# A two-layer decoder trunk: the first gate/up products queued behind the whole output projection, and a norm's matmuls queued one product later

## The chip, the core and the metric

One program runs on one core of one Trainium2 chip. Its engines work side by side, each on its own queue in program order: TensorE (PE for matrix products, with the loading of its stationary operand shown apart as PEld), VectorE (DVE), ScalarE (ACT), GpSimd (POOL) and SyncE (SP, which here only issues transfers). The metric is the device time of one execution in microseconds (us); lower is better.

## What is computed

A trunk of two layers over 512 tokens of width 1024, all in 32-bit floats. Each layer mixes tokens (attention of two kinds), adds the mix through an output projection, and adds a gated feed-forward block. The mixers matter here only as what comes before; the places of the change are the last two lines of the loop.

```python
for layer in range(2):
    mix = mixer(rmsnorm(x, attn_norm_g[layer]), ...)    # 512 x 1024
    x = x + mix @ w_out[layer]                          # output projection, 1024 x 1024
    h = rmsnorm(x, ffn_norm_g[layer])                   # the feed-forward norm
    g, u = jnp.split(h @ w_gate_up[layer], 2, axis=-1)  # 1024 x 5632
    x = x + (jax.nn.silu(g) * u) @ w_down[layer]        # 2816 x 1024
return rmsnorm(x, final_norm_g)
```

## The kernel before

**Products.** Every large matrix product is made from split operands: `hi` is the value rounded for TensorE, `lo` the rest, and a product is three matmuls (hi·hi, lo·hi, hi·lo). ACT makes `hi` (a cast), DVE makes `lo` (a subtraction). In the output projection two of the four weight pieces of a column block get `lo` in another way: ACT writes the negated weight and a POOL transfer adds to it.

**Output projection** (`out_proj`, `project`, lines 199 to 201). It works in four blocks of 256 output columns, `o` = 0 to 3, in the PSUM bank pairs `acc`, `sc`, `y`, `tr`. A block has 48 matmuls of 512 columns and uses four weight chunks (`whi`, `wlo`). After block `o` DVE adds the residual (lines 603, 604), ACT and DVE make the feed-forward operands of these columns: the split halves `xh`, `xl` and the sums `sh`, `sl` (line 608, `make`, lines 565 to 568, and `split`, lines 228 and 229). In layer 1 the new residual is also turned to token rows: four transposes for each 128 columns (line 619), which are traced one block later, and copied by ACT (line 620), with squares summed for the norm (line 625).

**Feed-forward** (`ffn`, `quad`). Eleven quads of 256 gate and 256 up columns. Each uses a seven-product scheme (a Strassen-like form): products `a11`, `s3`, `s2`, `s1`, `a22`, `a12`, `s4`, each with 24 matmuls of 256 columns (lines 835 to 837), in four contraction blocks `e` = 0 to 3, where `e` needs the columns that block `o = e` of the output projection made. For quad 0 the weights of the first three products are loaded and split ahead (`FirstThree`), and the first three products are traced in two parts: `e` = 0 to 2 of all three, then `e` = 3. They write the banks `acc`, `y` and `sc`, while block 3 of the projection writes `tr`. The down projection of an earlier quad fills places in later quads (`fill`, lines 934 to 936 in layer 1).

**The norm.** The products run on unnormalised operands; the row factor `r1` is multiplied in later (lines 900 and 902). In layer 0 it comes from `finish_norm`, in layer 1 from `norm_of_rows` (lines 630 to 638): a short chain on ACT and DVE, four products with a matrix of ones on PE (line 637), and a copy to `r1` on ACT (line 638).

**What sets the order.** The program is traced, and a scheduler then reorders each engine's instructions by its own model of their times, keeping the data dependences. `with behind(engine):` adds an edge: what the block traces on that engine stays behind the last instruction traced on it so far. On the chip each engine then runs its own row in the order given, and an instruction that waits holds all behind it.

Of the kernel before, what the change touches and what calls it, by code (L numbers as in the profile page):

```python
# [34 lines left out]
def tile_yoco(  # L35
# [68 lines left out]
    def behind(engine):  # L104

        e = engine.engine
        return tc.issue_after(next(i for i in reversed(nc.cur_bb.bb.instructions) if i.engine == e))
# [427 lines left out]
    NP = NKB // 2  # L535
# [91 lines left out]
    def norm_of_rows(ss):  # L627

        r = tmp("nrm", (P, NT))
        dve.tensor_add(ss[:, 0], ss[:, 0], ss[:, 1])  # L630
        rstd(ss[:, 0], NT, D, r)
        dve.tensor_scalar_mul(r, r, undo_k(D))
        d = work().rearrange("p (t c) -> p t c", c=P)
        b = bank("tr")
        for t in range(NT):
            dve.tensor_scalar_mul(d[:, t], ident, r[:, t : t + 1])
            pe.matmul(b[:, t * P : (t + 1) * P], ones, d[:, t], start=True, stop=True)
        act.copy(r1, b)
# [183 lines left out]
    def ffn(l, acc, last, qs, late, ring, sc, pl, ahead):  # L822
        raw, parts = ring.load, ring.parts
        wg = w_gate_up[l].rearrange("(e two p) c -> two p e c", two=2, p=P)
        wd = w_down[l].rearrange("(j p) c -> p j c", p=P)

        def product(b, form, w, es=range(NP)):

            hi, lo = w
            for u in range(2):  # L830
                o = b[:, u * H : (u + 1) * H]
                uc = slice(u * P, (u + 1) * P)
                for e in es:
                    ah, al = qs.operand(form, e)
                    pe.matmul(o, hi[:, e, uc], ah, start=u == 0 and e == 0, stop=False)  # L835
                    pe.matmul(o, lo[:, e, uc], ah, start=False, stop=False)  # L836
                    pe.matmul(o, hi[:, e, uc], al, start=False, stop=u == 1 and e == NP - 1)  # L837

        def halves(t):
            return t.rearrange("p (u c) -> p u c", u=2)  # L840

        gated = {}
        if last:
            ss = tmp("ss", (P, 2, NT))
            row_squares(qs.rows(), ss, 0)

        def quad(q, down):

            gc, uc = slice(q * 256, q * 256 + 256), slice(DFF + q * 256, DFF + q * 256 + 256)
            d = [next(down, None) for _ in range(4)]  # L850

            def fill(i):
                if d[i]:
                    d[i]()

            first, second = slice(0, H), slice(H, S)
            w = ahead[0] if q == 0 else FirstThree(l, q, ring)
            b11, t1 = w.b11, w.t1
            b21, b22 = raw(wg[1][:, :, gc]), raw(wg[1][:, :, uc])
            bp1, bp7, bp6 = bank("acc"), bank("y"), bank("sc")  # L860
            if q == 0:
                for es in (range(NP - 1), range(NP - 1, NP)):
                    product(bp1, "a11", w.w11, es)
                    product(bp7, "s3", w.wt3, es)
                    product(bp6, "s2", w.wt2, es)
                with behind(pe):
                    if last:
                        for f in late:
                            f()
                        row_squares(qs.rows(), ss, 1)  # L870
                    else:
                        finish_norm(acc, False, bank("tr"))
            else:
                product(bp1, "a11", w.w11)
                product(bp7, "s3", w.wt3)
                fill(0)
                product(bp6, "s2", w.wt2)
            p1, u2, u3 = sc.half("p1"), sc.half("u2"), sc.half("u3")
            g, u = sc.full("g"), sc.full("u")
            g1, g2, v1, v2 = g[:, :, first], g[:, :, second], u[:, :, first], u[:, :, second]  # L880
            act.copy(p1, bp1)
            dve.tensor_add(u2, bp6, p1)
            dve.tensor_add(u3, bp7, u2)
            bp5 = bank("acc")
            product(bp5, "s1", parts(t1))
            dve.tensor_sub(v2, halves(bp5), halves(u3))
            dve.tensor_sub(v1, halves(bp5), halves(u2))
            fill(1)
            if q == 0 and last:
                with behind(pe):  # L890
                    norm_of_rows(ss)
            dve.tensor_add(b11, b11, b21)
            bp4 = bank("y")
            product(bp4, "a22", parts(b11))
            dve.tensor_add(g2, halves(bp4), halves(u3))
            bp2 = bank("sc")
            product(bp2, "a12", parts(b21))
            dve.tensor_add(g1, halves(bp2), halves(p1))
            rr = r1.unsqueeze(1).to_broadcast([P, 2, S])
            dve.tensor_mul(g, g, rr)  # L900
            act.activation(g, g, AF.Silu)
            dve.tensor_mul(g, g, rr)
            fill(2)
            bp3 = bank(("acc", "y")[q % 2])
            product(bp3, "s4", parts(b22))
            dve.tensor_add(v1, halves(bp3), v1)
            fill(3)
            dve.tensor_mul(u, u, g)
            ah, al = (pl.tile([P, 2, S], F32R, tag=t, name=nm(t), bufs=4) for t in ("ah", "al"))
            split(u, ah, al)  # L910
            gated[q] = ah, al

        GROUPS = [(0,), (1, 2), (3, 4), (5, 6), (7, 8), (9, 10)]

        def blocks_of(group):
            return [(h[:, i], l_[:, i]) for q in group for h, l_ in (gated[q],) for i in range(2)]

        def down_blocks(group):

            k0, nk = 2 * group[0], 2 * len(group)  # L920
            w = {}

            def piece(i):
                a = blocks_of(group)
                c = i // 2
                if i % 2 == 0:
                    w[c] = parts(raw(wd[:, k0 : k0 + nk, c * 256 : c * 256 + 256], shape=(P, nk, 256)))
                hi, lo = w[c]
                b = bank("tr")
                if last:  # L930
                    for t in (2 * (i % 2), 2 * (i % 2) + 1):
                        tc_, o = slice(t * P, (t + 1) * P), b[:, (t % 2) * H : (t % 2) * H + H]
                        for k, (h, l_) in enumerate(a):
                            pe.matmul(o, h[:, tc_], hi[:, k], start=t % 2 == 0 and k == 0, stop=False)  # L934
                            pe.matmul(o, l_[:, tc_], hi[:, k], start=False, stop=False)  # L935
                            pe.matmul(o, h[:, tc_], lo[:, k], start=False, stop=t % 2 == 1 and k == nk - 1)  # L936
                    t0 = 2 * (i % 2)
                    dst = qs.rows()[:, t0 : t0 + 2, c * 256 : c * 256 + 256]
                    dve.tensor_add(dst, halves(b), dst)
                    return  # L940
                oc = slice((i % 2) * P, (i % 2) * P + P)
                for k, (h, l_) in enumerate(a):
                    pe.matmul(b, hi[:, k, oc], h, start=k == 0, stop=False)  # L943
                    pe.matmul(b, lo[:, k, oc], h, start=False, stop=False)  # L944
                    pe.matmul(b, hi[:, k, oc], l_, start=False, stop=k == nk - 1)  # L945
                if group != GROUPS[-1]:
                    dve.tensor_add(qs.block(i), b, qs.block(i))
                else:
                    xn = work()
                    dve.tensor_add(xn, b, qs.block(i))  # L950
                    split(xn, xh[:, i], xl[:, i])
                    squares(xn, nacc, i == 0)

            return [lambda i=i: piece(i) for i in range(8)]

        def all_down():
            for group in GROUPS[:-1]:
                yield from down_blocks(group)

        down = all_down()  # L960
        for q in range(NFF // 2):
            quad(q, down if q else iter(()))
        for f in down:
            f()
        exp_ln_tables()
        if not last:
            nacc = tmp("xacc")
            for f in down_blocks(GROUPS[-1]):
                f()
            return nacc  # L970
        k0 = 2 * GROUPS[-1][0]
        w = [[parts(raw(wd[:, k0 + k : k0 + k + 2, e * 512 : e * 512 + 512], shape=(P, 2, 512))) for k in (0, 2)] for e in range(2)]
        final(w, blocks_of(GROUPS[-1]), qs.rows(), ring, sc)
# [264 lines left out]
```

## Time and profile before

| | before |
|---|---|
| median of 3 runs | 1202.2 us (1201.6 to 1202.57) |
| profiled execution: time, span | 1206.7 us, 1204.9 us |
| mean granted clock of TensorE | 0.991 of 2.4 GHz |
| PE busy | 1168.8 us (97%) |
| PEld busy | 1064.8 us (88%) |
| DVE busy | 993.7 us (82%) |
| ACT busy | 662.8 us (55%) |
| POOL busy | 159.1 us (13%) |

The profiled execution took 1206.7 us, 4.5 us (0.4%) more than the median; its span runs from the first to the last instruction, and 1.8 us lie around it. Busy time is a sum of instruction durations, so an engine that is busy 97% of the span can still have stretches in which it stands still: these matter here. Layer 0's output projection ends near 273 us and its feed-forward runs to about 620 us; layer 1's output projection ends near 850 us and its feed-forward runs to the end.

### The profile page before, as it was taken

The page shows a single profiled execution, that of the slowest core. Times are in us where ns is not written, and L with a number is a line of the kernel's source. Part 1 is how long each engine was busy: PE and PEld are TensorE (multiplying, and loading weights), DVE is VectorE, ACT ScalarE, POOL GpSimd, SP SyncE. Part 2 cuts the span into 40 slices and gives each one's busy share as a digit, 9 for nine tenths or more (in the row PEclk, how much of TensorE's full clock was granted, in tenths as well). Part 3 has the DMA queues.
Part 4 walks back from the last instruction along what each step waited for, and adds up shares of the span by engine and source line. Part 5 has one row for each costly group of instructions (what it writes and reads, how often), then busy time and mean ns, then how long its engine had stood idle before and what let it go on. Part 6 is the DMA issues. An engine that isn't in the chain of part 4 may idle for free.

```text
span 1204.9 us, 21021 instructions
## 1 busy us (share of the span) xinstructions
PE 1168.8 (97%) x7854; PEld 1064.8 (88%) x7854; DVE 993.7 (82%) x1708; ACT 662.8 (55%) x1207; POOL 159.1 (13%) x154
## 2 busy tenths in 40 slices
PE   8999999999999999999999999997999999999997
PEld 7888888779999999999887888876899999999996
DVE  5879987789997787778789999977699878777776
ACT  7658776665443333333456979776554333333334
POOL 0002001121221111110001020112121111111000
PEclk9999999999999999999999999998999999999999
DMA  7533233466786666664133234455668666656512
GB/s 237 143 84 88 72 84 97 126 142 157 177 204 162 154 153 157 153 154 120 57 111 115 76 103 121 105 148 106 157 158 199 162 148 158 152 144 152 148 53 88
DMA packets 163065, 160.46 MB, mean 133 GB/s; under 512 B 12993, under 2 KB 152698, under 8 KB 162962
## 3 DMA queue, kind: packets, MB, share of 16 engines
q1 hardware_dynamic: 136722, 131.83, 36.7%
q0 software_dynamic: 26240, 27.27, 15.7%
q8 instruction: 62, 1.02, 0.4%
q14 instruction: 41, 0.34, 0.1%
HBM read 142.23 MB, written 2.10 MB: 120 GB/s over the span
## 4 chain that ended last, share of the span: by engine, by line
PE 74%; DVE 10%; ACT 5%; DMA 5%; issue 4%; SPq 1%; POOL 0%; ACTq 0%; DVEq 0%; POOLq 0%
PE acc L837 4%; PE acc L835 4%; PE acc L836 4%; PE y L837 4%; PE y L836 4%; PE y L835 4%; PE tr L943 3%; PE tr L944 3%; PE tr L945 3%; PE sc L836 3%; PE sc L837 3%; PE sc L835 3%; PE tr L936 3%; PE tr L934 3%; PE tr L935 3%
## 5 line engine op out<-in xcount | busy, mean ns | idle before, releaser
L228 ACT CAST fhi<-raw 128x1024 fp32r<-128x1024 f32 (+1 forms) x202 | 208.1, 1034 | 283.4 <-PE sc L837 100.9
L229 DVE TENSOR_TENSOR flo<-raw,fhi 128x1024 fp32r<-128x1024 f32 (+1 forms) x202 | 241.2, 1198 | 33.5 <-ACT fhi L228 33.4
L797 POOL DMA_DIRECT2D raw<-in_w_gate_up_dram x88 | 107.4, 1455 | 472.1 <-DMA raw<-in_w_gate_up_dram 288.5
L170 ACT ACTIVATE whi<-raw,gains 128x256 fp32r<-128x256 f32 (+1 forms) x192 | 86.6, 503 | 38.6 <-PE acc L201 22.0
L835 PE MATMUL acc<-xh,fhi 128*128 128x256 f32 x352 | 100.2, 285 | 5.6 <-ACT xh L228 5.6
L837 PE MATMUL acc<-xl,fhi 128*128 128x256 f32 x352 | 100.2, 285 | 0.6 <-DVE xl L229 0.5
L171 DVE SCALAR_TENSOR_TENSOR wlo<-raw,gains,whi 128x256 fp32r<-128x256 f32 (+1 forms) x192 | 87.2, 493 | 16.4 <-ACT whi L170 14.7
L836 PE MATMUL acc<-xh,flo 128*128 128x256 f32 x352 | 99.2, 282 | 0.0
L936 PE MATMUL tr<-flo,ah 128*128 128x256 f32 x288 | 81.3, 282 | 0.0
L934 PE MATMUL tr<-fhi,ah 128*128 128x256 f32 x288 | 81.1, 282 | 0.0
L935 PE MATMUL tr<-fhi,al 128*128 128x256 f32 x288 | 81.1, 282 | 0.0
L835 PE MATMUL y<-sh,fhi 128*128 128x256 f32 x256 | 72.7, 284 | 1.7 <-ACT sh L228 1.7
L835 PEld LDWEIGHTS acc<-xh,fhi 128*128 128x128 f32 x352 | 67.2, 191 | 7.0 <-ACT xh L228 6.5
L837 PE MATMUL y<-sl,fhi 128*128 128x256 f32 x256 | 72.8, 284 | 0.2 <-DVE sl L229 0.2
L836 PE MATMUL y<-sh,flo 128*128 128x256 f32 x256 | 72.6, 284 | 0.0
L943 PE MATMUL tr<-ah,fhi 128*128 128x512 f32 x176 | 69.2, 393 | 0.0
L944 PE MATMUL tr<-ah,flo 128*128 128x512 f32 x176 | 69.1, 393 | 0.0
L945 PE MATMUL tr<-al,fhi 128*128 128x512 f32 x176 | 68.8, 392 | 0.0
L837 PEld LDWEIGHTS acc<-xl,fhi 128*128 128x128 f32 x352 | 67.1, 191 | 1.6 <-DVE xl L229 1.4
L836 PEld LDWEIGHTS acc<-xh,flo 128*128 128x128 f32 x352 | 67.3, 191 | 0.4
L199 PE MATMUL acc<-xh,whi 128*128 128x512 f32 x168 | 66.7, 398 | 0.2 <-DVE qk L732 0.2
L200 PE MATMUL acc<-xh,wlo 128*128 128x512 f32 x168 | 66.3, 395 | 0.0
(482 smaller groups left out, 3787.6 us busy)
## 6 DMA issues: line engine op xcount, KB each, us to landing
raw<-in_w_gate_up_dram SPq DMA_DIRECT2D x220, 256.0 KB, 3.3
raw<-in_w_gate_up_dram POOLq DMA_DIRECT2D x88, 256.0 KB, 5.9
raw<-in_w_down_dram SPq DMA_DIRECT2D x80, 256.0 KB, 3.7
raw<-in_w_out_dram SPq DMA_DIRECT2D x32, 256.0 KB, 3.2
raw<-in_a_w_in_dram SPq DMA_DIRECT2D x48, 128.0 KB, 2.3
raw<-in_w_kv_shared_dram SPq DMA_DIRECT2D x24, 256.0 KB, 3.2
raw<-in_w_mem_kv_dram SPq DMA_DIRECT2D x16, 256.0 KB, 3.0
raw<-in_a_w_in_dram SPq DMA_DIRECT2D x16, 256.0 KB, 3.8
```

The lines of the kernel that those rows point to most:

```text
L228: act.copy(h, src)
L229: dve.tensor_sub(l, src, f32(h))
L797: pool.dma_start(t[:, k : k + 2], plus[:, k : k + 2], accum_op=ALU.add)
L835: pe.matmul(o, hi[:, e, uc], ah, start=u == 0 and e == 0, stop=False)
L836: pe.matmul(o, lo[:, e, uc], ah, start=False, stop=False)
L837: pe.matmul(o, hi[:, e, uc], al, start=False, stop=u == 1 and e == NP - 1)
L934: pe.matmul(o, h[:, tc_], hi[:, k], start=t % 2 == 0 and k == 0, stop=False)
L935: pe.matmul(o, l_[:, tc_], hi[:, k], start=False, stop=False)
L936: pe.matmul(o, h[:, tc_], lo[:, k], start=False, stop=t % 2 == 1 and k == nk - 1)
L943: pe.matmul(b, hi[:, k, oc], h, start=k == 0, stop=False)
L944: pe.matmul(b, lo[:, k, oc], h, start=False, stop=False)
L945: pe.matmul(b, hi[:, k, oc], l_, start=False, stop=k == nk - 1)
```

## The change

For quad 0 of both layers, the first three products now stand inside `with behind(pe):`, so that they stay behind the last instruction traced on PE, which belongs to the output projection. In layer 1 (`last`), `norm_of_rows` is traced after the product `a22` and no longer ahead of it, and stays behind that.

```diff
             if q == 0:
-                for es in (range(NP - 1), range(NP - 1, NP)):
-                    product(bp1, "a11", w.w11, es)
-                    product(bp7, "s3", w.wt3, es)
-                    product(bp6, "s2", w.wt2, es)
+                with behind(pe):
+                    for es in (range(NP - 1), range(NP - 1, NP)):
+                        product(bp1, "a11", w.w11, es)
+                        product(bp7, "s3", w.wt3, es)
+                        product(bp6, "s2", w.wt2, es)
                 with behind(pe):
                     if last:
                         for f in late:
...
             fill(1)
-            if q == 0 and last:
-                with behind(pe):
-                    norm_of_rows(ss)
             dve.tensor_add(b11, b11, b21)
             bp4 = bank("y")
             product(bp4, "a22", parts(b11))
             dve.tensor_add(g2, halves(bp4), halves(u3))
+            if q == 0 and last:
+                with behind(pe):
+                    norm_of_rows(ss)
             bp2 = bank("sc")
```

What this does to the rows of the engines, in three places. In the rows, `tr_9641` and `tr_9642` are the two banks of the projection's block 3 in layer 1, `acc_9798`, `y_9799` and `sc_9800` the banks of quad 0's first three products, `whi`, `wlo` weight pieces of the projection and `fhi`, `flo` those of the feed-forward.

**Layer 1, end of the projection, on PE.** Before, behind block 2 and its transposes:

```order
L619 MATMUL tr_9615<-ident,u_1794_9518 128x128 x4
L835 MATMUL acc_9798<-xh,fhi_9656 128x256
L836 MATMUL acc_9798<-xh,flo_9657 128x256
L837 MATMUL acc_9798<-xl,fhi_9656 128x256
L835 MATMUL acc_9798<-xh,fhi_9656 128x256
L836 MATMUL acc_9798<-xh,flo_9657 128x256
L835 MATMUL y_9799<-sh_9319,fhi_9660 128x256
L836 MATMUL y_9799<-sh_9319,flo_9661 128x256
L837 MATMUL y_9799<-sl_9320,fhi_9660 128x256
L199 MATMUL tr_9641<-yh_b,whi_9671 128x512
L199 MATMUL tr_9642<-yh_b,whi_9671 128x512
L837 MATMUL acc_9798<-xl,fhi_9656 128x256
```

and in the changed kernel at the same place:

```order
L619 MATMUL tr_9615<-ident,u_1794_9518 128x128 x4
L199 MATMUL tr_9641<-yh_b,whi_9671 128x512
L199 MATMUL tr_9642<-yh_b,whi_9671 128x512
L200 MATMUL tr_9641<-yh_b,wlo_9672 128x512
L201 MATMUL tr_9641<-yl_b,whi_9671 128x512
L200 MATMUL tr_9642<-yh_b,wlo_9672 128x512
L201 MATMUL tr_9642<-yl_b,whi_9671 128x512
```

Before, 30 of the 72 matmuls of quad 0's first three products stood ahead of the row `L200 tr_9641<-yh_b,wlo_9672` (8 ahead of the two L199 rows, 22 behind them); now none does, and all 72 follow the projection's last matmul and the eight transposes of block 2. The rows of ACT and DVE are the same as before up to the work that follows block 3.

**Layer 1, the norm, on PE.** Before, the four products with ones (`L637`) stood in quad 1's first product, near its end:

```order
L835 MATMUL acc_10084<-xh,fhi_10065 128x256
L836 MATMUL acc_10084<-xh,flo_10066 128x256
L637 MATMUL tr_9943<-work_9942,ones 128x128 x4
L837 MATMUL acc_10084<-xl,fhi_10065 128x256
```

now they stand in quad 0's last product:

```order
L835 MATMUL acc_10017<-sh_9319,fhi_10018 128x256
L836 MATMUL acc_10017<-sh_9319,flo_10019 128x256
L637 MATMUL tr_9974<-work_9973,ones 128x128 x4
L837 MATMUL acc_10017<-sl_9320,fhi_10018 128x256
L835 MATMUL acc_10017<-sh_9319,fhi_10018 128x256
```

Although the block is traced later, the row moved 21 matmuls towards the front of PE's row.

**Layer 0, end of the projection, on PE** (a piece of the difference; `tr_3311` and `tr_3312` are block 3's banks):

```order
 L199 MATMUL tr_3311<-yh_a,whi_3396 128x512
 L199 MATMUL tr_3312<-yh_a,whi_3396 128x512
-L835 MATMUL acc_3451<-xh,fhi_3326 128x256
-L836 MATMUL acc_3451<-xh,flo_3327 128x256
-L837 MATMUL acc_3451<-xl,fhi_3326 128x256
-L835 MATMUL acc_3451<-xh,fhi_3326 128x256
-L836 MATMUL acc_3451<-xh,flo_3327 128x256
-L837 MATMUL acc_3451<-xl,fhi_3326 128x256
-L835 MATMUL acc_3451<-xh,fhi_3326 128x256
-L836 MATMUL acc_3451<-xh,flo_3327 128x256
 L200 MATMUL tr_3311<-yh_a,wlo_3397 128x512
 L201 MATMUL tr_3311<-yl_a,whi_3396 128x512
```

Eight matmuls that stood between the last weight piece's `whi` and `wlo` rows now follow the projection.

## Rows read from the trace of the kernel before

**Rows 1.** Windows: stretch, its length, busy time by engine, granted clock, DMA share, GB/s

```profile
876.00:1180.00 304.00, 304.00 (x2541) 302.81 (x2540) 248.97 (x264) 122.74 (x124) 43.43 (x36) 1.00 0.59 144
```

**Rows 2.** Timeline of PE, layer 1, 823 to 850 us: start, duration, instruction, [idle before <-releaser]

```profile
823.75 0.28 PE L837 MATMUL acc<-xl,fhi 128*128 128x256 f32 x1
828.57 0.58 PE L835 MATMUL acc<-xh,fhi 128*128 128x256 f32 x1 [4.54 <-ACT xh L228]
...
829.81 1.05 PE L199 MATMUL tr<-yh_b,whi 128*128 128x512 f32 x2
...
839.19 0.50 PE L200 MATMUL tr<-yh_b,wlo 128*128 128x512 f32 x1
...
849.75 0.39 PE L201 MATMUL tr<-yl_b,whi 128*128 128x512 f32 x1
```

**Rows 3.** Timeline of all engines, the ACT and DVE rows ahead of the weight piece

```profile
823.44 1.05 ACT L228 CAST fhi<-raw 128x1024 fp32r<-128x1024 f32 x1 [4.50 <-DMA raw<-in_w_gate_up_dram]
...
825.03 0.69 DVE L229 TENSOR_TENSOR xl<-g,xh 128x512 fp32r<-128x512 f32 x1 [4.21 <-ACT xh L228]
...
828.42 1.05 ACT L620 COPY res<-tr 128x512 f32<-128x512 f32 x2
...
838.45 1.29 DVE L166 TENSOR_TENSOR wlo<-raw,whi 128x512 fp32r<-128x512 f32 x2
```

**Rows 4.** Windows: around that wait, around an earlier one, and around the norm's

```profile
823.30:828.60 5.30, 0.76 (x8) 0.55 (x6) 3.57 (x6) 5.16 (x9) 0.00 (x0) 1.00 0.42 67
828.60:839.20 10.60, 7.94 (x30) 6.46 (x30) 10.54 (x20) 9.16 (x19) 0.89 (x1) 0.52 0.17 52
...
872.00:876.00 4.00, 1.93 (x17) 1.85 (x17) 3.96 (x11) 1.63 (x2) 0.01 (x1) 1.00 0.52 151
...
210.00:214.00 4.00, 2.16 (x10) 1.50 (x10) 3.88 (x6) 3.15 (x7) 1.74 (x2) 1.00 0.88 216
214.00:218.00 4.00, 4.00 (x18) 3.30 (x16) 1.07 (x3) 1.73 (x3) 0.87 (x1) 0.57 0.32 73
```

**Rows 5.** Timeline of PE, transposes and the part e = 3 behind the projection

```profile
850.22 0.66 PE L619 MATMUL tr<-ident,u 128*128 128x128 f32 x4
850.63 0.36 PE L837 MATMUL y<-sl,fhi 128*128 128x256 f32 x1
...
851.66 0.65 PE L619 MATMUL tr<-ident,p 128*128 128x128 f32 x4
...
856.04 0.28 PE L837 MATMUL acc<-xl,fhi 128*128 128x256 f32 x1
856.58 0.39 PE L835 MATMUL acc<-xh,fhi 128*128 128x256 f32 x1 [0.26 <-ACT xh L228]
856.80 0.28 PE L836 MATMUL acc<-xh,flo 128*128 128x256 f32 x1
857.44 0.39 PE L837 MATMUL acc<-xl,fhi 128*128 128x256 f32 x1 [0.36 <-DVE xl L229]
```

**Rows 6.** Timeline of ACT, DVE and PE at layer 1's norm

```profile
868.37 1.05 ACT L228 CAST fhi<-raw 128x1024 fp32r<-128x1024 f32 x1 [2.38 <-DMA raw<-in_w_gate_up_dram]
...
872.56 0.68 DVE L906 TENSOR_TENSOR u<-acc,u 128x512 f32<-128x512 f32 x1
...
873.23 0.68 DVE L229 TENSOR_TENSOR flo<-raw,fhi 128x512 fp32r<-128x512 f32 x1
...
874.15 1.16 PE L637 MATMUL tr<-work,ones 128*128 128x128 f32 x8 [2.07 <-DVE work L636]
```

**Rows 7.** Timeline of PE, layer 0: waits at the projection's end and behind it

```profile
270.81 0.51 PE L200 MATMUL tr<-yh_a,wlo 128*128 128x512 f32 x1 [0.21 <-DMA wlo<-raw]
...
300.21 0.39 PE L836 MATMUL sc<-sh,flo 128*128 128x256 f32 x1 [0.44 <-DVE flo L229]
```

**Rows 8.** Timeline of ACT and PE, the first down projection of layer 1

```profile
883.65 1.05 ACT L228 CAST ah<-u 128x1024 fp32r<-128x1024 f32 x1 [0.63 <-DVE u L908]
...
885.17 0.41 PE L934 MATMUL tr<-fhi,ah 128*128 128x256 f32 x2
```

## The prediction

> **What bounds the kernel now.** I read the windows first. Over the last 300 us [rows 1] PE is busy all the time, and so is its weight load: 302.81 of 304.00 us. 2541 matmuls in 304 us make 0.1196 us for one, nearly all of 256 columns. So whatever is late on PE when this stretch begins is late at the end, and whatever PE does earlier comes off the end. A page of the Trainium skill bears on this reading (Perfetto Trace Analysis, Identifying the Most-Contended Engine): matmul busy time alone is a poor measure of how near PE is to its limit, and the share of weight loading is a better one. By the first alone some of the lateness could still be hidden; by the second, 99.6%, none can, and that is how I price it.
>
> The question is then what PE loses before 876 us. The timeline of PE shows its longest stop of the whole kernel at layer 1's output projection [rows 2]: a feed-forward product waits 4.54 us for `xh`, and from there to 839.19 us PE works in bits, until the projection's first `wlo` is there. The timeline of ACT and DVE shows why [rows 3]: ACT's cast waits for a weight transfer until 823.44 us, the cast of `xh` comes behind it, DVE has waited for that until 825.03, and from there DVE goes through a row of sums and splits without a pause worth naming, with the two subtractions that make `wlo` near its end, at 838.45 us. The first of them is done near 839.1 us.
>
> **The change, part by part.** The rows of ACT and DVE up to block 3's residual add are the same in both kernels, and nothing in that stretch of them waits for a feed-forward product. So I expect the first `wlo` at the same 839.1 us. Before, PE used the wait for 30 of the first three products' 72 matmuls. Now their place is behind the projection: PE has only the two L199 matmuls, which wait for the bank copies of ACT (828.42 us and on, [rows 3]), and stands still for the rest.
>
> 1. *Products moved out of the wait.* 30 x 0.1196 us [rows 1] = **3.6 us** later. Their cover is gone whole: the wait itself stays as long.
>
> 2. *The clock.* Before, PE at 828.6 to 839.2 us had a mean granted clock of 0.52 after the 4.54 us stop [rows 2, 4], so nearly all of it at the lower of the two levels, 1.2 GHz; but it was mostly waiting, so little was lost. Now a stop of some 15 us, broken by two matmuls, comes right ahead of 46 matmuls that have nothing to wait for, so they should start at 1.2 GHz. The price from rows: at the other stop of the kernel, before 214 us, the next 4 us of work ran at 0.57 [rows 4], that is (1 - 0.57) x 4 x 2 = 3.4 us at the lower level, which costs half of it, **1.7 us**. Bounds: nothing (after the norm's wait of 2.07 us the clock stayed at 1.00, [rows 4, 6]), and half of the 10.2 us that the low stretch of 828.6 to 839.2 us held, 5.1 us. I take 1.7, because as in the row at 214 us PE is then fed without a break. The Trainium skill has the same rule of halves (TensorE: Matmul & The Clock Gate, Terms: the penalty is the throttled time times one minus the ratio of the clock). Put on the stretch that this very place shows, it would give 5.1 us and a sum of 7.1 us in place of 3.7; no row here shows PE fed without a break and still slow for so long.
>
> 3. *Transposes without cover.* The 46 matmuls end as before about 0.23 us behind their last start [rows 2], later by the clock's 1.7 us. Then come two groups of four transposes. Each needs a bank that DVE frees with the residual add. Before, the first group starts at 850.22 and the second at 851.66 us, with products between [rows 5]; the first group takes 0.41 us (850.22 to 850.63). Now nothing stands between: PE waits 850.22 - 849.98 = 0.24 and 851.66 - 850.63 = 1.03 us, together **1.3 us**.
>
> 4. *Waits for block 3's operands.* Before, from 849.98 us to the norm's wait (which begins at 874.15 - 2.07 = 872.08 us, [rows 6]) PE takes 22.1 us for 155 matmuls (18.5 us at the pitch of [rows 1]) and 16 transposes (1.6 us at 0.41 for four). The other 2.0 us are waits for the part `e` = 3, which comes from the projection's last block; two of them show as gaps in the starts, 856.04 to 856.58 and 856.80 to 857.44 us, 0.9 us over the pitch [rows 5]. Now 54 matmuls (6.5 us) stand ahead of `e` = 3, and these waits go, except for small joins: **-1.6 us** (bounds: -0.9 and -2.0).
>
> 5. *The norm.* PE reaches L637 at 872.08 + 3.6 + 1.7 + 1.3 - 1.6 = 877.1, less the 21 matmuls by which the row moved up (2.5 us): 874.6 us. Its operand hangs on a transfer of quad 1's weights, for which ACT waits until 868.37 us [rows 6]; the transfers of that ring queue on SP behind the end of the projection, so they come 1.7 us later. From there to L637 it took 5.8 us. Two DVE instructions of that stretch, line 906 and a 512-wide `flo` (0.6 us each from start to start), follow the norm in the new row of DVE: 4.6 us. 868.37 + 1.7 + 4.6 = 874.7 us. So PE and operand come together, and the wait of 2.07 us all but goes: **-2.0 us** (bounds: -2.07; and -0.8 if the chain keeps its 5.8 us). The second half of the change thus does on PE the opposite of what its place in the program says, and costs nothing by itself.
>
> 6. *Layer 0.* Eight matmuls move out of a wait for the last `wlo`, a transfer that lands at the same time [rows 7]: 8 x 0.1196 = 0.95 us. Behind it PE stands 0.44 us for a DVE split [rows 7], which may hide as much. Between 0.5 and 0.95 I take **0.7 us**; DVE's chain to that split starts from PE's own products and so moves along.
>
> Nothing is loaded or computed more or less, and no transfer is added: DMA costs nothing beyond step 5.
>
> Sum: 3.6 + 1.7 + 1.3 - 1.6 - 2.0 + 0.7 = **+3.7 us**. The profiled execution of 1206.7 us (a span of 1204.9 and 1.8 us around it) would become 1210.4; it lies 4.5 us above the median, so I carry the difference to the median: 1202.2 + 3.7 = **1205.9 us**.
>
> **The rivals.**
> *Harder (a new wait takes the old one's place), 1208.2 us.* The norm's chain keeps its 5.8 us, +1.2, and the first down products wait. In the new row of PE these stand 71 matmuls behind L637, before 84. Before, from L637 to the end of the cast of `ah` it took 883.65 + 1.05 - 874.15 = 10.5 us [rows 8]; now PE comes there 0.9 + 71 x 0.1196 = 9.4 us behind it. If that chain keeps its length too, PE waits 1.1 us: 1205.9 + 2.3. For it: PE found `ah` with only 0.5 us to spare (885.17 us). Against it: both chains lose a split or two in DVE's new row.
>
> *Hidden, 1203.5 us.* The clock stays up (-1.7) and layer 0's part is swallowed (-0.7). That also stands for a change that does next to nothing. For it: the clock stayed at 1.00 after 2.07 us. Against it: this stop is several times longer, and it fell after 4.54 us.
>
> *Faster, 1196.5 us.* The projection was held up by the products ahead of it, and block 3 runs inside the wait. From the L199 rows at 829.81 us its 46 matmuls (849.98 - 839.19 = 10.8 us) would end at 840.6 in place of 849.98, and the 30 products follow: -9.4 + 3.6 = -5.8. The point that decides is the first `wlo`: each us that it is ready ahead of 839.1 gives one back, and from about 835.4 us on the change gains. For it: `whi` is there early, and PE's row stands behind `xh` in [rows 2]. Against it: DVE makes `wlo` at 838.45 us, and its row is the same.
>
> **Chances and range.** Likeliest 0.57 (its own range 1204.2 to 1207.8 from the bounds of clock, norm and layer 0), harder 0.17, hidden 0.20, faster 0.06. The range reaches into hidden and harder: 1202.9 to 1209.0. What a measurement of this kernel can tell from no change is about 0.2%, 2.4 us. Slower by more: nine tenths of the likeliest and all of the harder case, 0.69; within it 0.25; faster 0.06.
>
> **What the new profile would show.** Step 1: one PE wait of over 9 us that ends at the projection's first L200, released by DVE `wlo`, and DVE's L166 within half a us of 838.45 (plus layer 0's shift). Step 2: a granted clock near half for the first 3 to 4 us behind it. Step 3: waits of 0.2 and 1 us at L619. Step 4: no waits for `xh`, `xl` behind them. Step 5: L637 with a wait under 0.5 us. Step 6: a wait over 1 us for layer 0's last `wlo`. The prediction is wrong if `wlo` comes early, if PE waits again for `ah` or `al` near 884 us, or if stops show anywhere between 876 and 1180 us.

## The result and the profile after

The changed kernel took 1210.0 us (median of 4, 1209.1 to 1210.6), the kernel before 1202.4 us (median of 4): a ratio of 1.0063, 95% interval 1.0046 to 1.0081, so +5.5 to +9.7 us. The sign was forecast, the place was forecast, the size was not: 1210.0 lies 1.0 us above the range, and +7.65 is more than twice the +3.7 of the sum. Two later measurements of the same kernel, with more executions, gave +4.65 and +4.37 us (below). So there are two things to explain: what the change costs, and why the first number and the sum are so far apart.

The timeline of PE in the changed kernel, at the places of [rows 2, 5, 6, 8] (start us, length, engine, line, operation, output<-input, count, idle time ahead and its releaser):

```profile
823.46 0.60 PE L619 MATMUL tr<-ident,u 128*128 128x128 f32 x4
828.53 1.28 PE L199 MATMUL tr<-yh_b,whi 128*128 128x512 f32 x2 [4.48 <-ACT res L620]
838.67 0.80 PE L200 MATMUL tr<-yh_b,wlo 128*128 128x512 f32 x1 [8.86 <-DVE wlo L166]
839.26 0.63 PE L201 MATMUL tr<-yl_b,whi 128*128 128x512 f32 x1
...
851.50 0.40 PE L201 MATMUL tr<-yl_b,whi 128*128 128x512 f32 x1
851.98 0.66 PE L619 MATMUL tr<-ident,u 128*128 128x128 f32 x4
853.42 0.66 PE L619 MATMUL tr<-ident,p 128*128 128x128 f32 x4 [0.79 <-DVE u L603]
853.83 0.36 PE L835 MATMUL acc<-xh,fhi 128*128 128x256 f32 x1
...
874.52 1.13 PE L637 MATMUL tr<-work,ones 128*128 128x128 f32 x8 [0.15 <-DVE work L636]
...
884.00 0.39 PE L935 MATMUL tr<-fhi,ah 128*128 128x256 f32 x1
```

The stop that [rows 2] showed with 30 products in it is now empty: 4.48 us for ACT's bank copies, 1.28 us of work, 8.86 us for the first `wlo`. It ends at the `wlo`, not at a product. No wait for `xh` or `xl` is left behind it, and the norm's is 0.15 us.

ACT and DVE, which set that point, as in [rows 3]:

```profile
822.92 1.05 ACT L228 CAST fhi<-raw 128x1024 fp32r<-128x1024 f32 x1 [3.60 <-DMA raw<-in_w_gate_up_dram]
837.93 1.29 DVE L166 TENSOR_TENSOR wlo<-raw,whi 128x512 fp32r<-128x512 f32 x2
882.90 1.04 ACT L228 CAST ah<-u 128x1024 fp32r<-128x1024 f32 x1
```

From the cast to `wlo` it takes 15.01 us, to the hundredth what it took before (838.45 - 823.44).

The windows of the changed kernel, as in [rows 1, 4] (busy time and count of PE, PEld, DVE, ACT, POOL, then the granted clock, DMA share, GB/s):

```profile
823.90:838.60 14.70, 1.43 (x4) 0.58 (x2) 14.03 (x24) 13.25 (x27) 0.89 (x1) 0.59 0.24 57
838.60:842.60 4.00, 3.93 (x9) 3.15 (x10) 1.49 (x3) 0.81 (x2) 0.86 (x1) 0.50 0.70 126
843.60:847.60 4.00, 4.00 (x19) 3.24 (x18) 0.00 (x0) 0.00 (x0) 0.00 (x0) 0.99 0.00 0
876.00:1180.00 304.00, 304.00 (x2553) 303.68 (x2552) 248.69 (x265) 122.21 (x125) 43.48 (x36) 1.00 0.60 146
```

Block 3 starts at a granted clock of 0.50, the lower level (9 matmuls in 4 us; 19 in the 4 us from 843.6 us at 0.99), and behind 876 us there is again no slack. Layer 0's wait for its last `wlo` grew from 0.21 us [rows 7]:

```profile
267.78 0.50 PE L200 MATMUL tr<-yh_a,wlo 128*128 128x512 f32 x1 [1.31 <-DMA wlo<-raw]
```

### The profile page after: what moved, and what is told of

Read it like the earlier page. It is cut to its first block, busy times and chain, and to the rows that moved or that the text cites. A ratio compares the mean times of both kernels' runs of the same rounds, so it can differ in the third digit from the quotient of the medians.

```text
span 1207.9 us, 21022 instructions
## 1 busy us (share of the span) xinstructions
PE 1166.7 (97%) x7854; PEld 1063.2 (88%) x7854; DVE 995.3 (82%) x1708; ACT 663.3 (55%) x1207; POOL 158.7 (13%) x154
## 4 chain that ended last, share of the span: by engine, by line
PE 75%; DVE 8%; ACT 6%; DMA 6%; issue 4%; SPq 1%; POOL 0%; ACTq 0%; DVEq 0%; POOLq 0%
PE acc L837 4%; PE acc L836 4%; PE acc L835 4%; PE y L837 4%; PE y L835 4%; PE y L836 4%; PE tr L944 3%; PE tr L945 3%; PE tr L946 3%; PE sc L836 3%; PE sc L837 3%; PE sc L835 3%; PE tr L935 3%; PE tr L937 3%; PE tr L936 3%
## 5 line engine op out<-in xcount | busy, mean ns | idle before, releaser
L935 PE MATMUL tr<-fhi,ah 128*128 128x256 f32 x288 | 81.3, 282 | 0.0
L199 PE MATMUL acc<-xh,whi 128*128 128x512 f32 x168 | 66.5, 397 | 0.2 <-DVE qk L732 0.2
L200 PE MATMUL acc<-xh,wlo 128*128 128x512 f32 x168 | 66.3, 394 | 0.0
```

## The experiments

Versions that were measured together share the executions of the kernel before: the same median of it marks them. Those executions lie between 1198.9 and 1208.1 us, far wider than the 1201.6 to 1202.9 of the first four. The ratio is an estimate of its own and not the quotient of the two medians; the two differ most for layer 1 only (1.0008 against 1.0024).

| run | median us (executions) | kernel before beside it (executions) | ratio, 95% interval |
|---|---|---|---|
| norm only | 1202.8 (12) | 1203.8 (29) | 0.9993 (0.9976 to 1.001) |
| layer 0 only | 1204.0 (12) | 1203.8 | 0.9998 (0.9985 to 1.001) |
| layer 1 only | 1206.65 (11) | 1203.8 | 1.0008 (0.9995 to 1.002) |
| `wlo` first | 1199.6 (6) | 1203.8 | 0.9949 (0.9933 to 0.9965) |
| changed kernel again | 1209.0 (5) | 1204.3 (11) | 1.0032 (1.0020 to 1.0044) |
| first edit, both layers | 1210.4 (6) | 1204.3 | 1.0049 (1.0035 to 1.0063) |
| `wlo` first, on the kernel before | 1195.2 (5) | 1204.3 | 0.9924 (0.9912 to 0.9936) |
| casts last | 1194.3 (5) | 1204.3 | 0.9911 (0.9898 to 0.9923) |
| 105 matmuls in the stop | 1210.9 (6) | 1203.95 (16) | 1.0061 (1.0041 to 1.008) |
| changed kernel, third time | 1208.3 (11) | 1203.95 | 1.0038 (1.0025 to 1.005) |
| casts last, on the kernel before | 1196.2 (6) | 1203.95 | 0.9935 (0.9915 to 0.9955) |
| 56 matmuls in the stop | 1206.15 (12) | 1204.25 (17) | 1.0019 (1.0005 to 1.0032) |

**The norm alone.** Only the second hunk of the diff:

```diff
-            if q == 0 and last:
-                with behind(pe):
-                    norm_of_rows(ss)
             dve.tensor_add(b11, b11, b21)
...
             dve.tensor_add(g2, halves(bp4), halves(u3))
+            if q == 0 and last:
+                with behind(pe):
+                    norm_of_rows(ss)
```

> Only the norm moves; the products stay ahead of the projection's end. In this kernel the row of every engine, PE, DVE, ACT, SP and POOL, is the same as in the kernel before, instruction by instruction (only buffer numbers differ). So both theories expect 1202.4 us, within 0.7. It is run for its trace. The traces of before and after lie 3.0 us apart, the medians 7.65 us, so 4.6 us are not accounted for. Theory A (the profiled execution of before lost 4.5 us at a place that the change does not touch): this trace has a span near 1200.6 us, and against the profiled before the rows gain in stretches far from the two projection ends. Theory B (the gap sits at the change): against the profiled before the rows gain the 4 to 5 us between 820 and 880 us or between 260 and 305 us.

No difference, as both theories had it. Its trace is a second execution of the rows of before, and PE's waits there differ from the profiled ones (who waited for whom: us in total, times, longest):

```profile
PE acc L835 <- ACT xh L228: 4.9, 3, 3.9
PE y L835 <- ACT sh L228: 1.7, 1, 1.7
PE acc L837 <- DVE xl L229: 0.7, 2, 0.4
PE tr L637 <- DVE work L636: 0.4, 1, 0.4
PE y L837 <- DVE sl L229: 0.2, 1, 0.2
```

The norm's wait, 2.07 us in [rows 6], is 0.4 us here on the same rows (0.8 us in the trace of the next run). Its span is 1202.4 us, 2.5 us under the profiled one. 2.4 us lie around 214 us, at a place that the change doesn't touch: from the DVE instruction that starts at 207.33 us in the profiled execution to the one at 224.07 us that execution took 16.74 us, this one 14.38, and every other trace 14.3 to 15.5. There PE waited 1.84 us for a transfer in the profiled execution and 1.09 here, and the next 4 us had a clock of 0.57 there and 1.00 here. Another 1.7 us are the norm's wait, and other stretches of this trace are longer. So the gain lies elsewhere than at the change, as theory A had it, though the span is 1.8 us over the 1200.6 it named; the norm's wait is the exception.

**Layer 0 alone, layer 1 alone.** The first hunk with a condition:

```diff
-                with behind(pe):
+                with behind(pe) if not last else nullcontext():
```

and `if last` for the other, the norm at its old place in both.

> Only layer 0's eight products move behind the projection. My sum: +0.7 us (0.5 to 0.95); the trace of after shows +1.1 between 259 and 304 us. So 1203.0 to 1203.5 us. Theory B for this place: if the missing 4.6 us sit here, 1207 to 1208 us.

> Only layer 1's products move behind the projection; the norm stays where it was traced. My sum: products +3.6, clock +1.7, transposes +1.3, waits for the last part -1.6, norm -2.0 (here the norm's place in PE's row is again late, so its wait goes for the lateness instead) = +3.0: 1205.4 us. Theory B for this place: +6.5 to +7: 1209 us, with the first wait near 823 us shorter in the kernel before than its profiled execution shows.

Neither time shows more than the sum had (+0.2 us where it had +0.7, and +2.85 where it had +3.0; by the ratios -0.2 and +1.0); theory B, that 4 us more sit at one place, is out for both. The first edit in both layers with the norm untouched:

> The products behind the projection in both layers, the norm left where it was traced. Against the changed kernel the norm's product stands at the same place of PE's row but for one matmul, and DVE and PE differ in 12 and 16 rows behind it. Theory 1 (the second edit costs and gives nothing by itself): the same as the changed kernel within 1 us, and PE's wait at the norm under 0.5 us here too. Rival (the second edit is what costs): 2 us or more below the changed kernel.

It came out 1.4 us above the changed kernel, where theory 1 had at most 1, with intervals that overlap; the rival, that the second edit is what costs, is out. Its trace has its lateness in layer 0 (66.99 us in the stretch that is measured below, where the others have 62 to 65), not in layer 1.

**`wlo` first.** The point that was to decide the rival "faster" is moved. In layer 1 quad 0's weights are traced behind the block's weights:

```diff
-            if o == 3:
+            if o == 3 and l == 0:
                 ahead()
             project([(w_out[l], o * 256, 256)], None, yh, yl, bs, NKB, order=order, by_dma=(0, 4))
+            if o == 3 and l == 1:
+                ahead()
```

> The changed kernel, and in layer 1 the feed-forward weights made ahead are traced behind the last block of the projection and no longer ahead of it. DVE's row then has the first wlo as the second instruction behind its long wait (825 us and not 838). Theory 1 (the projection's first wlo is what the change leaves standing bare): PE's stop ends near 829 us with the bank copies, the projection ends 8 to 10 us earlier than in after, near 842 us, and the time is 1200 to 1203 us, no slower than before. Rival (the operands of the last part, or the weights that are now later, end last anyway): the projection ends early, but the products behind it wait, and the time stays above 1207 us.

```profile
819.00 0.69 DVE L166 TENSOR_TENSOR wlo<-raw,whi 128x512 fp32r<-128x512 f32 x1
...
821.61 0.62 ACT L181 CAST whi<-raw 128x512 fp32r<-128x512 f32 x1 [3.97 <-DMA raw<-in_w_out_dram]
...
825.67 0.50 PE L199 MATMUL tr<-yh_b,whi 128*128 128x512 f32 x1 [4.32 <-ACT res L622]
826.01 0.39 PE L200 MATMUL tr<-yh_b,wlo 128*128 128x512 f32 x1
```

DVE makes `wlo` at 819 us, the stop of 8.86 us is gone, and the time is 4.2 us under the kernel before beside it: theory 1 (0.4 us under the range that it named), and the rival above 1207 us is out. The same swap without holding the products:

> The kernel before with the same swap as in the last run: layer 1's feed-forward weights are traced behind the projection's last block, the products are not held behind it. The row of PE then keeps 8 of the products ahead of the block, where before 30 stood. Theory 1 (what decides is when the first wlo comes, and products ahead of it only fill what is left of the wait): 3 to 5 us under the kernel before, and within 1.5 us of the version with the products held behind. Rival (holding them behind is what gained there): the same as the kernel before.

1195.2 us, 9.1 us under before: more than the 3 to 5 expected, and by the ratios (0.9924 against 0.9949, with intervals that touch) no worse than the version with the products held. So it was not holding them that gained. (In its trace 4 products stand ahead of the block and 3 within it, not 8 ahead.) The last 4.32 us of the stop in the version with the products held are ACT's bank copies, which stand behind the cast shown at 821.61 us, which waits for a transfer. The edit, against that version:

```diff
-            if o == 3 and l == 1:
-                ahead()
             for f in late:
                 f()
             late = []
+            if o == 3 and l == 1:
+                with behind(act):
+                    ahead()
```

> The changed kernel with layer 1's feed-forward weights traced behind the bank copies of block 2 too, and held behind them on ACT. PE's remaining stop of the last swap was 4.32 us for the bank copies of ACT, which stood behind a cast that waits for a transfer; now the casts of quad 0's weights come behind them. Theory 1 (each us that block 3 starts earlier comes off the end): the stop shrinks to under 1 us, and the time is 2 to 4 us below the last swap's 1199.6, near 1196. Rival (the weights' splits become what the products wait for): PE stands 3 us or more at its first feed-forward products, and the time is 1199 to 1204.

```profile
820.92 0.68 DVE L166 TENSOR_TENSOR wlo<-raw,whi 128x512 fp32r<-128x512 f32 x1
...
825.68 0.50 PE L199 MATMUL tr<-yh_b,whi 128*128 128x512 f32 x1 [1.44 <-ACT res L623]
...
840.91 0.80 PE L838 MATMUL acc<-xh,fhi 128*128 128x256 f32 x2 [1.62 <-ACT fhi L228]
```

1194.3 us, 0.9% under the kernel before and the lowest median of all; its interval lies clear of `wlo` first (0.9949), but overlaps that of `wlo` first on the kernel before (0.9924). The stop is 1.44 us, not under 1. Part of the rival is there too: 1.62 us at the first product, for its weights. Moving the casts alone, on the kernel before, gives layer 1 the same row of PE: the products fall behind the projection there without being held. So it is this version without layer 0's part:

> The version with the casts last, without layer 0's part of the change. Its rows differ from that version in layer 0's eight matmuls and in two rows of DVE. By the stretches of the traces layer 0's part costs 0.9 us: 1193.4 us, where the version with the casts last had 1194.3; by the rival (layer 0's part is free, as its run alone had it with +0.2): the same, 1194.3.

1196.2 us, higher than either had it; the ratio of 0.9935 has an interval that overlaps that of 0.9911: not told apart.

**The changed kernel again.**

> The changed kernel itself, in as many executions as the experiments. 29 executions of the kernel before on one chip lay between 1198.9 and 1208.1 us (median 1203.8), so a median of three or four is good to 2 or 3 us only. Theory 1 (my sum, with layer 1 alone at +2.85 and layer 0 alone at +0.2 us): +3 to +4.5 us over the kernel before of the same call. Theory 1b (the norm's credit of 2.0 us was a wait that only the profiled execution had; two others of the same rows show 0.4 and 0.8 us): +4.5 to +5.5. Rival (the first measurement stands, +7.65): +7 to +8.

> The changed kernel once more, as the partner of the run with 105 more matmuls and for more executions. By the stretches of the traces (layer 1 +3.4 to +3.9, layer 0 +0.9): +4.3 to +4.8 us over the kernel before of this call. If the first measurement is nearer: +7 to +8.

+4.65 and +4.37 us by the medians, +3.9 and +4.6 by the ratios: the sum by the traces, not the first measurement.

**The clock.** 105 matmuls that nothing reads are put into the stop, behind the first L199 matmul:

```diff
                     pe.matmul(o, hi[:, k, c], ah[:, kb, :n], start=first, stop=False)
+                    if fill and first and j == 0:
+                        with behind(pe):
+                            for _ in range(fill):
+                                pe.matmul(spare[:, :H], hi[:, k, c], ah[:, kb, :H], start=True, stop=True)
```

> The changed kernel with 105 more matmuls of 256 columns in the stop of layer 1's projection, into a bank that nothing reads. They stand ahead of the two L199 matmuls and wait for nothing: 105 x 0.12 = 12.6 us of the 14.8 us between the transposes and the first wlo. The rest of the program is the same. Theory 1 (the stop lets the clock fall, and that costs 2.3 us: 46 matmuls take 13.06 us from the first start to the last where they took 10.79): the first matmul behind the stop runs at the full clock, the 46 take 10.8 us, and the time is 2 to 2.3 us below the changed kernel of this call. Rival (the clock's fall is made good later, by a wait that is shorter): the 46 take 10.8 us, but the time is the changed kernel's within 0.7 us.

```profile
826.56 0.79 PE L200 MATMUL tr<-yh_b,whi 128*128 128x512 f32 x1 [3.31 <-ACT res L625]
827.15 14.73 PE L204 MATMUL acc<-yh_b,whi 128*128 128x256 f32 x105
841.72 0.39 PE L205 MATMUL tr<-yh_b,wlo 128*128 128x512 f32 x1
```

This run missed: it came out 2.6 us above the changed kernel. I had the extra matmuls ahead of the two L199; they stand behind the first of them (L200 in this kernel) and end 5 us after the `wlo`. The block behind them took 10.70 us from its first L205 to its last L206. With 56 of them:

> The run with extra matmuls again, with 56 in place of 105. There they stood behind the first L199 matmul and not ahead of it, ran from 827.15 to 841.72 us, and so ended 5.0 us behind the first wlo (835.98 + 0.7 us); the 46 matmuls behind them took 10.8 us at the full clock, and the time was 2.6 us over the changed kernel, which is 5.0 - 2.3. With 56 they end some 0.5 to 1 us ahead of the wlo. Theory 1 (the clock's fall in the stop costs 2.3 us of the end): the 46 take 10.8 us, and the time is 2.3 us below the changed kernel's +4.4 over the kernel before: +2.1 us (1.2 to 3). Rival (what is saved is lost again at the norm or behind it): +4.4 as the changed kernel, with a wait at the norm of 1.5 us or more.

```profile
828.52 8.01 PE L204 MATMUL acc<-yh_b,whi 128*128 128x256 f32 x56
838.10 0.50 PE L205 MATMUL tr<-yh_b,wlo 128*128 128x512 f32 x1 [1.33 <-DVE wlo L166]
...
848.66 0.40 PE L206 MATMUL tr<-yl_b,whi 128*128 128x512 f32 x1
...
871.69 1.13 PE L642 MATMUL tr<-work,ones 128*128 128x128 f32 x8 [0.16 <-DVE work L641]
```

From the first L200 to the last L201 of the block (here L205 and L206) PE takes 10.56 us, as before the change, where the changed kernel takes 12.58 to 12.83. So the trace shows the clock's part, and it is not given back at the norm (0.16 us). The time is +1.9 us, against +4.4, which fits; by itself it shows less, for the two were not measured together and their intervals (1.0005 to 1.0032, 1.0025 to 1.005) overlap.

## Why the prediction was right or wrong

What the change costs in layer 1, from the starts of four instructions in each trace: ACT's cast behind its wait for a weight transfer, the first L200 and the last L201 of block 3, and L637.

| us | before | norm only | layer 0 only | changed | again | third | 56 matmuls |
|---|---|---|---|---|---|---|---|
| cast to first L200 | 15.75 | 15.99 | 16.06 | 15.75 | 15.76 | 15.76 | 15.78 |
| to last L201 | 10.56 | 11.27 | 10.55 | 12.83 | 12.60 | 12.58 | 10.56 |
| to L637 | 24.40 | 22.99 | 23.37 | 23.02 | 23.03 | 23.02 | 23.03 |
| of that, wait at L637 | 2.07 | 0.36 | 0.76 | 0.15 | 0.15 | 0.16 | 0.16 |
| cast to L637 | 50.71 | 50.25 | 49.98 | 51.60 | 51.39 | 51.36 | 49.37 |

L637 moved up by 21 matmuls (2.5 us), so the changed kernel has 53.9 to 54.1 us for the same work: +3.2 to +3.4 against the profiled execution of before, +3.8 to +4.0 against the two others with its rows in layer 1 (mean 50.1). Layer 1 only and the first edit in both layers have 51.5 from the cast to L637, as the changed kernel. Layer 0, from DVE's sum of line 565 that starts at 252.43 us in the profiled before to its add of quad 1 at 315.02 us: 62.0 to 63.2 us in five traces with the products ahead (median 62.5), 62.6 to 67.0 in nine with them behind (median 63.2), +0.7. Together about +4.6 us, and the two larger measurements say +4.65 and +4.37.

Layer 1's part by the terms of the sum (the first is 30 products at the pitch of [rows 1] in each column, and the 21 matmuls by which L637 moved up are put back):

| us | forecast | against the profiled before | against the mean of the two others |
|---|---|---|---|
| products | +3.6 | +3.6 | +3.6 |
| length of the wait itself | 0 | 0 | -0.3 |
| clock | +1.7 | +2.0 to +2.3 | +1.7 to +1.9 |
| transposes and waits for `e` = 3 | -0.3 | -0.5 | -0.8 |
| norm | -2.0 | -1.9 | -0.4 |
| together | +3.0 | +3.2 to +3.4 | +3.8 to +4.0 |

1. *Products, +3.6: right.* The wait itself stays as it was (15.75 us from cast to L200 in both, 15.99 and 16.06 in the two others) and all of its cover is gone.
2. *The clock, +1.7: right in kind, 0.3 to 0.6 us small against the profiled before.* 12.83 - 10.56 = 2.27 us in the profiled execution, 2.0 us in the two others, and with the stop filled the block takes 10.56 us again. The price came from a stretch of 4 us at 0.57 elsewhere; here the first 4 us are at 0.50 and the low level lasts a little longer. With the products ahead the block did not always start at the upper level either: in the trace of the norm alone its first 4 us had 0.73, and it took 11.27 us.
3. and 4. *Transposes +1.3 and waits for `e` = 3, -1.6: right together.* From the last L201 to L637 without its wait: 22.33 us before, 22.87 - 9 x 0.1196 (30 products more, 21 fewer) = 21.79 after, -0.54 where I had -0.3. The waits at L619 (851.98 less 851.73, which is the last start at 851.50 and the 0.23 us of the prediction, makes 0.25; the second is 0.79 us) are near the 0.24 and 1.03 forecast, and no wait for `xh` or `xl` is left.
5. *The norm, -2.0: right for the two traces, by luck, and wrong as a price.* L637 starts at 874.52 us (forecast 874.7) behind a wait of 0.15, but by another path. The forecast had the cast ahead of the norm's chain wait for its transfer until 868.37 + 1.7 = 870.07 us, and 4.6 us from there. In the changed kernel that cast starts at 867.99 us without a wait, and it is 6.53 us from there to L637: the two instructions did leave DVE's row ahead of the norm, but another `flo` and a sum came in. The two errors cancel. And what is saved is a wait that only the profiled execution had in full: 0.36 and 0.76 us in the two others. In the kernel before the transfer does set it: ACT waited 2.38, 0.67 and 1.07 us for the transfer in the three traces, each time 0.31 us more than PE at L637. The casts ahead of the norm's chain (changed kernel, norm only, layer 0 only; [rows 6] has the profiled before):

```profile
867.99 1.04 ACT L228 CAST fhi<-raw 128x1024 fp32r<-128x1024 f32 x1
865.79 1.05 ACT L228 CAST fhi<-raw 128x1024 fp32r<-128x1024 f32 x1 [0.67 <-DMA raw<-in_w_gate_up_dram]
862.95 1.05 ACT L228 CAST fhi<-raw 128x1024 fp32r<-128x1024 f32 x1 [1.07 <-DMA raw<-in_w_gate_up_dram]
```

What the change gains there is 0.2 to 0.6 us; a wait on a transfer in one profile is a draw, not a property of the row. I also put the norm's new place down to the second half of the change: the second hunk alone moves no row of any engine, and with the first hunk alone L637 moves up by 22 matmuls, one more than in the changed kernel. It is the first edit that moved it.
6. *Layer 0, +0.7: agrees* (+1.08 in the two traces, 0.7 in the medians), but the traces of the two kinds overlap (62.6 us in that of layer 0 only), and its run alone had +0.2 us: it is not shown apart from the noise.

*Harder* did not come: L935 starts at 884.00 us, 0.06 us behind the end of the cast of `ah` (882.90 + 1.04), without a wait; that cast ends 9.4 us behind L637, no longer 10.5. So it was missed by very little. *Hidden* is out by the 8.86 us stop and the clock. *Faster* named the right condition: with the first `wlo` early, the held products stand in a kernel that is faster than before.

**Two steps failed, and both took one draw for the kernel.** One is term 5 of the sum, "the wait of 2.07 us all but goes: -2.0 us": the lower bound of its gain was 0.8, and the runs show 0.2 to 0.6 us in its place, because the kernel before waits there only as long as its transfer is late. Of that miss of 1.6 us the wait's own length (-0.3) and the transposes and waits (0.5 less than forecast) hid half. The other is the last step of the sum, "so I carry the difference to the median: 1202.2 + 3.7". The profiled execution lay 4.5 us above three executions that agreed within 1 us, and I took those three for the kernel's time. In 73 later executions, in four groups, the kernel before has medians of 1203.8 to 1204.3 us. From 1204 the same sum gives 1207.7; with the terms as measured (+4.6) it gives 1208.6, and the changed kernel measured 1209.0 and 1208.3. The range carried the bounds of the terms but nothing for the base, though the 4.5 us stood there to be seen.

So of the 4.1 us between 1205.9 and 1210.0 the base is 1.8, the terms 0.9, and 1.4 are left. The base doesn't explain the difference of +7.65, for the kernel before measured beside it had 1202.4: of that, 3.0 us are in no trace.

What stays open is why the first measurement had the kernel before at 1202.4 and the changed one at 1210.0, some 1.6 us under and 1 to 1.7 us over the later ones. Two of its four executions of the changed kernel lie above 1210.0, and one of the 16 later ones does; all four of the kernel before lie at or under 1202.92, as 22 of the 73 later ones do. So a draw of four that went both ways at once is possible but unlikely, and nothing here shows another cause.

## What to carry to other kernels

Here PE ran its row in order and had no slack behind the stop. The 30 products were free ahead of the wait and cost 3.6 us behind it, and the emptied wait cost 1.7 to 2.3 us of clock on top. But the larger gain, 4 to 10 us, was to look at what the wait is for, and to let the engine that makes it (here DVE's split of the first weights, then ACT's copies) do that first. Price a saved wait only if a second execution of the same rows shows it, above all where a transfer ends it. Where the profiled execution and the timed median differ by more than the effect forecast, the base belongs in the range.

## What was not expected of the hardware

Stops of PE of like length left different clocks. In the profiled before a stop of 1.84 us that ended at 213.68 us was followed by 4 us at 0.57 [rows 4]; in the changed kernel the stop at the same place was 2.16 us and the clock stayed at 1.00, as its windows show:

```profile
212.70:216.70 4.00, 3.98 (x26) 3.51 (x26) 2.31 (x8) 2.59 (x7) 0.87 (x1) 1.00 0.41 93
```

The stop of 1.44 us in the version with the casts last did not lower it either (first line), but in the same trace it was down behind two stops of 0.79 and 1.62 us with four transposes between them, at the first product (second line), and so it was behind the 4.32 us in the version with `wlo` first (third line):

```profile
826.00:830.00 4.00, 4.00 (x19) 3.21 (x18) 2.96 (x5) 4.00 (x10) 0.31 (x1) 1.00 0.59 106
841.00:844.00 3.00, 3.00 (x14) 3.00 (x15) 3.00 (x3) 2.05 (x3) 0.00 (x0) 0.50 0.93 280
826.00:830.00 4.00, 4.00 (x12) 3.13 (x11) 4.00 (x9) 4.00 (x12) 1.18 (x2) 0.57 0.31 54
```

And one program on one chip spread over 9 us (29 executions, 1198.9 to 1208.1 us). The traces show part of such a spread in stretches that end in transfers: the wait of ACT for one weight transfer in layer 1 was 4.50 and 3.88 us in two traces of the rows of before, and 3.60, 3.83 and 4.76 us in three of the changed kernel.
